# Weights' tiles at other offsets in the on-chip memory: one layer of a hybrid trunk on one core

## The chip, the cores and the metric

The kernel runs on one core of a Trainium2 chip. A core has TensorE (matrix products, results into PSUM), VectorE, ScalarE and GpSimd (elementwise work), SyncE (it issues most transfers), and SBUF, an on-chip memory of 128 partitions, in which a tile occupies the same bytes of every partition. "Offset" below is a tile's first byte in a partition, taken modulo 256. The metric is the device time of one execution in microseconds (us); the profile shows one such execution, with every instruction of every engine.

## The reference

The reference computes one layer on 1024 frames of 1024 channels, and a last RMSNorm. Cut to its large products:

```python
h = rmsnorm(x, norm_mix_g)
proj = h @ w_in                                  # 1024 -> 9248 columns
o_a = gated_delta_rule_chunked(q_a, k_a, v_a, g_a, beta_a)    # 8 heads of 128, after a short convolution
y_a = (rmsnorm(o_a, gdn_norm_g) * silu(gz)) @ w_branch_gdn
o_b = gla_chunked(q_b, k_b, v_b, log_fg)                      # 4 heads, 128 key and 256 value channels
y_b = (rmsnorm(o_b, gla_norm_g) * silu(lr)) @ w_branch_gla
x = x + (sigmoid(gate_a) * y_a + sigmoid(gate_b) * y_b) @ w_out
# cross-attention on 256 memory tokens, 4 heads of 256
x = x + (softmax(q @ k.T / 16) @ v) @ xattn_wo
x = x + square(relu(rmsnorm(x, norm_mlp_g) @ mlp_w1)) @ mlp_w2   # 4096 inner channels
return rmsnorm(x, norm_final_g)
```

All inputs and the output are float32.

## The kernel before

**Products in three steps.** Each large product is made of fp32r matmuls, a matmul form that takes float32 words. Both operands are split into a high part and a remainder, and three matmuls add up in PSUM: high x high, high x remainder, remainder x high (`mm3`, lines 493, 495 and 497). A matmul has a stationary operand of 128 x 128, loaded ahead of it by a separate weight load (PEld in the profile), and a moving operand of 512 or 256 columns that streams through. Most products go through a Strassen-Winograd scheme with seven products of half-size blocks in place of eight (`wino`, `gla_dense`).

**The weights' tiles.** A block of weights is loaded from HBM into a tile named raw. `split` (lines 531 to 534) makes its high part by a copy on ScalarE and the remainder by a subtraction on VectorE or GpSimd. The parts go into tiles of 4096 bytes a partition:

- wop, in a ring of four slots, in the pools w1 (first phases: memory keys and values, gates, GLA) and w4 (merge, output, attention, MLP);
- whi and wlo, two slots each, in the pool w2 (the delta-rule phase); wlo also in the first phase's own pool.

Four slots of a ring lie one behind the other. Every tile that is asked for under one name ("tag") takes the next slot that is free. In most products the weights are the stationary operand. In the GLA values (line 884), the folded output weights (line 711) and the scores of two of the four attention heads (line 1916) a weights' tile is the moving operand instead.

**Where tiles lie.** Pools are stacked from the left or from the right end of SBUF, and small "pad" tiles (`pad`, line 440) fill up a pool's size, so that in the built program all tiles of activations and weights of 2 KB and more have offset 0. A few others don't: gst, in which the first phase collects results for a transfer, at 96; rmb at 96; the gate weights w2g at 64; the GLA state S at 224; the identity matrix at 128.

**What sets the order.** The program is built twice. In the first pass a planner (`Plan`) takes the recorded instructions and simulates the engines with its own costs; in the second pass the order that it found is laid on each engine's queue. It takes tile sizes from `made_in` (line 449), to know which pools share memory.

Of the kernel before, what the change touches and what calls it, by code (L numbers as in the profile page):

```python
# [41 lines left out]
XO = (('K3', 'Q1', 'V0'), ('V0', 'V1', 'O2'))  # L42
LOVU = (5,)
LOV = (0, 2, 5)


def c3(t):
# [376 lines left out]
class Layer:  # L424
# [23 lines left out]

    def made_in(self, pool, shape, dt, tag, name, bufs):
        kw = {} if bufs is None else {"bufs": bufs}  # L450
        t = pool.tile(list(shape), dt, tag=tag, name=name, **kw)
        self.plan.tile(pool, tag, bufs, (t if isinstance(t, bass.AP) else t[:]).tensor.name, 4 * int(np.prod(shape[1:])))
        return t

    def psd(self):
# [1148 lines left out]

    def wino(self, bs, evicts, order=range(7), after=None, lov=LOV):

        n, ws = self.wino_w(order, lov)
        yield
        for i, p in enumerate(order):
            if i == (FW if len(ws) > 1 else 0):  # L1610
                self.fetch_w()
            for e, (w, evict) in enumerate(zip(ws, evicts)):
                x, w = bs[p], w[p]
                pt = self.psd() if (p + e) % 2 == 0 else self.pss()
                yield from self.mm3(pt, [((w[0][:, k], w[1][:, k]), (x[:, 0, k], x[:, 1, k])) for k in range(n)])
                evict(p, pt)
            if after:
                after(p)
# [360 lines left out]
    def phase_mlp(self, sp):  # L1979
# [9 lines left out]

        def up(us, order=range(7), after=None, lov=LOV):  # L1990
            puts = [self.spill(self.ad[u // 4], u % 4, nc.vector if u < 2 else None) if u < 15 else
                    lambda i, half, x: nc.sync.dma_start(self.ald[:, 2 * half + i], x) for u in us]
            return self.wino(self.mo, [self.sums(sp, relu2(put)) for put in puts],
                             order, after, lov)
# [335 lines left out]
```

## Time and profile before

| | |
|---|---|
| median of 3 runs | 2245.36 us (2243.86 to 2246.61) |
| the profiled execution | 2244.09 us |
| its span, first to last instruction | 2242.4 us |
| mean granted TensorE clock | 0.983 |
| HBM read, written | 212.35 MB, 85.75 MB |

In the profile, PE is TensorE's matmuls, PEld its weight loads, DVE VectorE, ACT ScalarE, POOL GpSimd. A group's line gives the source line, the engine, the operation, the tiles as out<-in with buffer numbers left out, and the shapes. TensorE is held by matmuls nearly throughout:

```profile
PE   7899999989899999999998999999999999999996
DVE  8835999697848858668557994558998778667756
ACT  6534554446445455355444433455675556544433
DMA  7832122122102102111167672234355445878732
```

Each digit is the busy share, in tenths, of one of 40 equal slices of the span; DMA is the mean share of the 16 DMA engines.

### The profile page before, as it was taken

To read this page: it belongs to the slowest core of one execution; us is meant where nothing else is said; L and a number is where in the kernel's file an instruction comes from. 1 tells how busy PE (TensorE), PEld (TensorE's weight loads), DVE (VectorE), ACT (ScalarE), POOL (GpSimd) and SP (SyncE) were. 2 spreads that over 40 slices of the span, in tenths; PEclk is the share of its full clock that TensorE was granted. 3 is DMA by queue.
4 is the path that set the end of the run, shared out by engine and by line. 5 is a ranking of instruction groups with operands and counts; after the bars stand their busy time and mean duration, and the time that the engine had idled before them with its cause. 6 is when DMAs were issued, how large, how long until landed. Compare 5 with 4: busy or idle time off the path is not lost.

```text
span 2242.4 us, 32240 instructions
## 1 busy us (share of the span) xinstructions
PE 2168.5 (97%) x11552; PEld 1861.4 (83%) x11552; DVE 1670.7 (75%) x2901; ACT 1106.3 (49%) x2223; POOL 369.7 (16%) x333
## 2 busy tenths in 40 slices
PE   7899999989899999999998999999999999999996
PEld 7788979878788888888886888998888888888886
DVE  8835999697848858668557994558998778667756
ACT  6534554446445455355444433455675556544433
POOL 2201112022212222121011320002331002000012
PEclk9999999999999999999999999999999999999998
DMA  7832122122102102111167672234355445878732
GB/s 257 303 132 73 58 72 72 49 74 86 62 25 93 54 29 99 38 48 67 43 215 249 213 271 90 95 132 139 125 200 167 155 155 172 275 243 283 244 122 81
DMA packets 148465, 300.23 MB, mean 134 GB/s; under 512 B 15816, under 2 KB 22344, under 8 KB 148304
## 3 DMA queue, kind: packets, MB, share of 16 engines
q1 hardware_dynamic: 141504, 289.75, 38.6%
q10 hardware_dynamic: 6800, 8.42, 1.1%
q8 instruction: 91, 1.49, 0.3%
q14 instruction: 70, 0.57, 0.1%
HBM read 212.35 MB, written 85.75 MB: 133 GB/s over the span
## 4 chain that ended last, share of the span: by engine, by line
PE 82%; DVE 10%; issue 3%; DMA 3%; ACT 2%; POOL 0%; SPq 0%; DVEq 0%; ACTq 0%; POOLq 0%
PE pd L493 19%; PE pd L495 19%; PE pd L497 19%; PE ps L495 5%; PE ps L493 5%; PE ps L497 5%; PE ps L565 2%; PE ps L1268 1%; PE ps L1259 1%; DVE Pm L1235 1%; DMA e<-obd 1%; DVE wop L534 1%; DVE pr L1233 1%; PE ps L1188 1%; PE ps L1325 1%
## 5 line engine op out<-in xcount | busy, mean ns | idle before, releaser
L533 ACT ACTIVATE wop<-raw 128x512 fp32r<-128x512 f32 (+1 forms) x444 | 297.2, 675 | 508.7 <-PE pd L497 235.9
L534 DVE TENSOR_TENSOR wop<-raw,wop 128x512 fp32r<-128x512 f32 (+1 forms) x383 | 293.6, 770 | 144.1 <-ACT wop L533 136.8
L534 POOL TENSOR_TENSOR wop<-raw,wop 128x512 fp32r<-128x512 f32 x27 | 38.8, 1438 | 389.0 <-ACT wop L533 235.5
L1129 DVE SCALAR_TENSOR_TENSOR acc<-cin,convw,acc 128x1024 f32<-128x1024 f32 x72 | 100.7, 1399 | 1.9 <-ACT acc L1127 0.7
L533 ACT ACTIVATE whi<-raw 128x512 fp32r<-128x512 f32 x86 | 52.0, 628 | 76.1 <-issue 34.8
L497 PE MATMUL pd<-t,wop 128*128 128x512 f32 x220 | 88.0, 400 | 0.0
L493 PE MATMUL pd<-t,wop 128*128 128x512 f32 x220 | 86.1, 391 | 0.8 <-ACT t L533 0.8
L495 PE MATMUL pd<-t,wop 128*128 128x512 f32 x220 | 85.9, 391 | 0.7 <-DVE t L534 0.7
L493 PE MATMUL pd<-B1a,wop 128*128 128x512 f32 (+1 forms) x220 | 82.6, 376 | 0.0
L497 PE MATMUL pd<-B1a,wop 128*128 128x512 f32 (+1 forms) x220 | 82.4, 375 | 0.0
L534 POOL TENSOR_TENSOR wlo<-raw,whi 128x512 fp32r<-128x512 f32 x29 | 45.4, 1569 | 197.7 <-ACT whi L533 143.5
L497 PE MATMUL pd<-A0a,wlo 128*128 128x512 f32 x172 | 68.8, 400 | 1.1 <-DVE wlo L534 1.1
L493 PE MATMUL pd<-A0a,whi 128*128 128x512 f32 x172 | 69.5, 404 | 0.0
L493 PE MATMUL pd<-A1b,whi 128*128 128x512 f32 x172 | 69.3, 403 | 0.0
L497 PE MATMUL pd<-A1a,wlo 128*128 128x512 f32 x172 | 68.4, 397 | 0.0
L495 PE MATMUL pd<-A1a,whi 128*128 128x512 f32 x172 | 68.3, 397 | 0.0
L497 PE MATMUL pd<-A1b,wlo 128*128 128x512 f32 x172 | 68.3, 397 | 0.0
L495 PE MATMUL pd<-A0b,whi 128*128 128x512 f32 x172 | 68.2, 396 | 0.0
L493 PE MATMUL pd<-A1a,whi 128*128 128x512 f32 x172 | 67.9, 395 | 0.0
L495 PE MATMUL pd<-A0a,whi 128*128 128x512 f32 x172 | 67.8, 394 | 0.0
L495 PE MATMUL pd<-A1b,whi 128*128 128x512 f32 x172 | 67.7, 393 | 0.0
L493 PE MATMUL pd<-A0b,whi 128*128 128x512 f32 x172 | 67.6, 393 | 0.0
(627 smaller groups left out, 7165.2 us busy)
## 6 DMA issues: line engine op xcount, KB each, us to landing
raw<-in_w_dram SPq DMA_DIRECT2D x120, 256.0 KB, 3.4
raw<-in_w_gdn_dram SPq DMA_DIRECT2D x64, 256.0 KB, 2.7
raw<-in_w_dram SPq DMA_DIRECT2D x32, 512.0 KB, 4.4
e<-ad SPq DMA_DIRECT2D x63, 256.0 KB, 4.8
ad<-q SPq DMA_DIRECT2D x45, 256.0 KB, 4.4
rawa<-ad SPq DMA_DIRECT2D x42, 256.0 KB, 4.9
A0b<-tgd SPq DMA_DIRECT2D x32, 256.0 KB, 5.8
ad<-acc SPq DMA_DIRECT2D x30, 256.0 KB, 2.4
```

What stands on the lines that cost most here:

```text
L493: nc.tensor.matmul(out, lh, rh, start=first and i == 0, stop=False)
L495: nc.tensor.matmul(out, lh, rl, start=False, stop=False)
L497: nc.tensor.matmul(out, ll, rh, start=False, stop=last and i == n - 1)
L533: nc.scalar.activation(hi, raw, AF.Copy)
L534: (lo_eng or nc.gpsimd).tensor_tensor(lo, raw, hi.bitcast(F32), SUB)
L565: self.nc.tensor.transpose(pt[:, i * P:(i + 1) * P], s, self.ident)
L1129: nc.vector.scalar_tensor_tensor(acc, cin[:, 1 + i:1 + i + T], cw[:, i:i + 1], acc, MUL, ADD)
L1188: nc.tensor.matmul(pt[:, i * P:(i + 1) * P], kc, kc, start=True, stop=True)
L1233: nc.vector.tensor_tensor(pr, X[:, c + 1:32, c:c + 1].broadcast_to([P, m, n]), Pm[:, c:c + 1, 0:n].broadcast_to([P, m, n]), MUL)
L1235: nc.vector.tensor_tensor(Pm[:, c + 1:32, 0:n], Pm[:, c + 1:32, 0:n], pr, ADD)
L1259: nc.tensor.matmul(pt[:, i * 96:(i + 1) * 96], NT[:, u + i, :], PF[:, v + i, 0:96], start=True, stop=True)
L1268: nc.tensor.matmul(pt[0:96, i * n:(i + 1) * n], PF[:, v + i, 0:96], Z, start=True, stop=True)
```

## The change

Tiles of three tags get some words more than they use: 24 (96 bytes) for wop, 16 (64 bytes) for whi and wlo. The extra words lie at a slot's end, and `made_in` returns a view of the tile without them. The planner is told the larger size.

```diff
+SHIFT = {"wop": 24, "whi": 16, "wlo": 16}
...
     def made_in(self, pool, shape, dt, tag, name, bufs):
         kw = {} if bufs is None else {"bufs": bufs}
-        t = pool.tile(list(shape), dt, tag=tag, name=name, **kw)
-        self.plan.tile(pool, tag, bufs, (t if isinstance(t, bass.AP) else t[:]).tensor.name, 4 * int(np.prod(shape[1:])))
+        n, more = int(np.prod(shape[1:])), SHIFT.get(tag, 0)
+        t = pool.tile([shape[0], n + more] if more else list(shape), dt, tag=tag, name=name, **kw)
+        self.plan.tile(pool, tag, bufs, (t if isinstance(t, bass.AP) else t[:]).tensor.name, 4 * (n + more))
+        if more and len(shape) == 3:
+            return t[:, :n].rearrange("p (a b) -> p a b", a=shape[1])
+        if more:
+            return t[:, :n].rearrange("p (a b c) -> p a b c", a=shape[1], b=shape[2])
         return t
```

The slots' distance becomes 4192 bytes for wop and 4160 for whi and wlo. In the built program the offsets are then:

| tiles | before | after |
|---|---|---|
| wop, four slots (pools w1, w4) | 0 | 64, 128, 160, 224 |
| whi, two slots (w2) | 0 | 0, 64 |
| wlo, two slots (w2) | 0 | 128, 192 |
| wlo, two slots (first phase) | 0 | 0, 64 |
| raw in w1 and w4, the input x, GLA's work tiles (ex, qk, v, sm), tiles of the first phase (acc, sq), tg of the gates' pool | 0 | 128 |
| gst, rmb | 96 | 224 |
| S, w2g | 224, 64 | 96, 192 |
| activations in A0a to B1b, t2 to t6, kv, mT, raw in w2, all tiles of the delta-rule phase of 512 bytes and more but jk | 0 | 0 |

Every engine's instructions stand in the same order as before.

## The prediction

> **What bounds the kernel now.** I read the page's busy shares first, then the chain of work that ended last.
>
> ```profile
> span 2242.4 us, 32240 instructions
> PE 2168.5 (97%) x11552; PEld 1861.4 (83%) x11552; DVE 1670.7 (75%) x2901; ACT 1106.3 (49%) x2223; POOL 369.7 (16%) x333
> PE 82%; DVE 10%; issue 3%; DMA 3%; ACT 2%; POOL 0%; SPq 0%; DVEq 0%; ACTq 0%; POOLq 0%
> ```
>
> TensorE is busy for 97% of the span and carries 82% of the chain; the transfers carry 3%. The change moves no instruction from one place to another, so the question is whether a matmul step, a split on ScalarE or VectorE, or a transfer gets longer or shorter when its operand begins at another address. Busy matmul times cannot answer that, because their ends are modelled. What can is the distance from one start to the next where nothing waits, read from the timeline of TensorE:
>
> ```profile
> 1403.16 0.39 PE L493 MATMUL pd<-B0a,wop 128*128 128x512 f32 x1
> 1403.39 0.39 PE L495 MATMUL pd<-B0b,wop 128*128 128x512 f32 x1
> 1403.61 0.39 PE L497 MATMUL pd<-B0a,wop 128*128 128x512 f32 x1
> ...
> 1405.65 0.39 PE L497 MATMUL pd<-B0a,wop 128*128 128x512 f32 x1
> 1405.88 0.39 PE L493 MATMUL pd<-B0a,wop 128*128 128x512 f32 x1
> ```
>
> The first column is the start in us. From 1403.16 to 1405.88 lie 12 steps, so a step of 512 columns is 2.72/12 = 226.7 ns. The names in front of the comma are the moving operand, the names behind it the weights. In the scores of the attention the roles turn, and a step has 256 columns:
>
> ```profile
> 1439.73 0.28 PE L495 MATMUL pd<-wop,t 128*128 128x256 f32 x1
> 1439.85 0.28 PE L497 MATMUL pd<-wop,B0a 128*128 128x256 f32 x1
> ...
> 1440.93 0.28 PE L497 MATMUL pd<-wop,B0a 128*128 128x256 f32 x1
> ```
>
> Ten steps in 1.20 us: 120 ns. So 256 more columns cost 106.7 ns (0.417 ns each), and 226.7 - 2 x 106.7 = 13.3 ns of every step do not depend on its length. In this program every operand of these matmuls begins at a multiple of 256 bytes. Counted in the built program, 7,152 steps are of the long form and 2,112 of the short one; 9,264 x 13.3 ns = 123 us of the span are this fixed part. It is the one thing in the profile that a collision between the reading of weights and the reading of the moving operand could be, and so the largest sum that the change can touch.
>
> **The change part by part.**
>
> *Order and waits.* Tile for tile, each engine issues the same instructions in the same order as before. At the head of the delta-rule phase a few small tiles now overlap the grown weights' pool of the phase before, so ScalarE and GpSimd each get one more wait ahead of an instruction, and one wait of VectorE (for two transfers) stands seven instructions earlier, ahead of the small vv at line 1174 instead of line 528.
>
> ```profile
> 529.36 0.15 DVE L1174 TENSOR_SCALAR vv<-ssk 128x8 f32<-128x8 f32 x1
> 531.88 0.17 DVE L528 TENSOR_TENSOR rs_o<-rs_y,rs_t 128x8 f32<-128x8 f32 x1
> ```
>
> What is awaited belongs to a pool that was left before this phase began, and the row of line 528 names no idle time and no releaser; I take 0. If the two transfers were late, at most the 2.5 us between these rows would be moved, with the key block of the first two heads queued behind. Bounds 0 to +2.5 us.
>
> *ScalarE and VectorE on shifted tiles.* 444 + 86 copies write hi tiles whose slots move, and in two of the three weights' pools the raw tiles that they read move to 128. Before, one tile of 2 KB, gst, begins 96 bytes past a multiple of 256; the same operation writes acc at 0:
>
> ```profile
> L533 ACT ACTIVATE wop<-raw x444: 611/632/1074, 4.0 to 2196.4; 128x512 fp32r<-128x512 f32 x131, 128x1024 fp32r<-128x1024 f32 x17
> L533 ACT ACTIVATE whi<-raw x86: 612/631/648, 493.8 to 1150.4; 128x512 fp32r<-128x512 f32 x86
> L534 DVE TENSOR_TENSOR wop<-raw,wop x383: 653/692/2315, 122.4 to 2191.7; 128x512 fp32r<-128x512 f32 x183, 128x1024 fp32r<-128x1024 f32 x9
> L715 ACT ACTIVATE gst<-pd,rs_o x16: 668/684/690, 81.5 to 131.1; 128x512 f32<-128x512 f32 x16
> L1127 ACT ACTIVATE acc<-pd,convw x48: 676/682/701, 507.4 to 1058.2; 128x512 f32<-128x512 f32 x48
> L701 DVE TENSOR_TENSOR gst<-pd,rmb x32: 406/410/426, 47.3 to 79.5; 128x256 f32<-128x256 f32 x32
> L686 DVE TENSOR_TENSOR kv<-pd,kv x16: 402/417/425, 17.4 to 122.1; 128x256 fp32r<-128x256 f32 x16
> ```
>
> Medians of 684 against 682 ns on ScalarE, and 410 against 417 on VectorE, where rmb is read and gst written off the grid and kv on it. The price is 0 to +2 ns a split; 530 x 2 ns = 1 us of engines that are 49% and 75% busy, and the copies of a unit are made while TensorE is on the one before. I take 0.
>
> *The moving operand off the grid.* The words ahead of the change say that the moving operands stay at 0. That holds for the long steps with activations as moving operand, but not everywhere: in the GLA values, the folded output weights and the scores of two heads the weights' tiles are themselves the moving operand; by the built program 1,136 steps stream from a shifted slot. One plain-fp32 matmul of before streams from an address 224 bytes past the grid (S in the GLA scan, line 1007), beside others that stream v from 0 with the same weights' shape:
>
> ```profile
> 486.30 0.59 PE L1005 MATMUL ps<-v,ex 128*128 128x256 f32 x2
> 486.73 0.59 PE L1007 MATMUL ps<-S,qk 128*128 128x256 f32 x2
> 487.16 0.59 PE L1003 MATMUL ps<-v,ex 128*128 128x256 f32 x2
> 487.59 0.59 PE L1005 MATMUL ps<-v,ex 128*128 128x256 f32 x2
> ```
>
> Each pair of records takes 0.43 us, whichever address it streams from. Bounds: 0 by this row, and one more fixed part (13.3 ns x 1,136 = 15 us) if the doubled rate of the fp32r stream has no slack left. I take 0.
>
> *The weights off the grid.* This is the main term. 6,352 long steps and 576 short ones load their weights from a slot that isn't at 0. The nearest row is again plain fp32: w2g, a stationary tile 64 bytes past the grid.
>
> ```profile
> 209.83 1.88 PE L931 MATMUL ps<-sm,w2g 96*128 96x512 f32 x4
> L931 PE MATMUL ps<-sm,w2g x16: 590/592/594, 209.8 to 435.2; 96*128 96x512 f32 x16
> ```
>
> Four records last 1.88 us from the first start to the last end, and one lasts 0.592, so three steps take 1.29 us: 0.43 us a step of 512 columns. The rows at 486 us give 0.43/2 = 0.215 us for 256 columns with weights at 0. Twice 0.215 is 0.43: within the 10 ns of these columns, shifted weights add nothing. The same rows speak against a gain: 256 columns at twice 0.417 ns are 213 ns, so with both operands at 0 plain fp32 pays only about 2 ns of fixed part a step. Equal residues alone therefore don't make the 13.3 ns; the fp32r form does.
>
> Bounds for a shifted step, then: -13.3 ns (the whole fixed part is a collision and goes) to +13.3 ns (the load takes twice its fixed part); 6,928 x 13.3 = 92 us either way. I take 0, by the nearest row.
>
> [...]
>
> *Transfers.* The raw tiles of two pools, x and the GLA work tiles now begin 128 past the grid. [...] From the chain's row alone: 3% of 2242 us are 67 us, and raw tiles are a part of it; I bound this at 0 to +4 us, one sixteenth, and take 0, because the weights are fetched several units ahead.
>
> **Sum.** 0 for each part. The profiled execution took 2244.1 us (span 2242.4 and 1.7 around it); the median of the runs is 2245.4, with 2.7 us between lowest and highest. I predict 2245 us.
>
> **Rivals.**
>
> *Slower: a load from an odd multiple of 32 bytes costs more.* Two of the four wop slots lie at 160 and 224. If such a load touches a row of the memory more than an aligned one, its fixed part grows; for half as much again, 6.7 ns, 2,464 long and 240 short steps give 18 us: 2263; for twice, 36 us: 2281. It decides from about 2 ns a load on, because these steps follow each other without a gap. With every shifted slot dear it is 92 us: 2337. [...] Against it: the w2g row, though at 64, never at an odd 32.
>
> *Slower by little: transfers, or the 1,136 streamed steps.* 4 to 15 us: 2249 to 2260.
>
> *Faster: the fixed part is a collision.* For it: it is constant, in both forms, and every operand sits at the same residue. If it goes on all 6,928 steps, 92 us x 82% of the chain = 76 us: 2169; if only where the residues differ enough, a part of that. Against it: the plain-fp32 rows, and that the step stays at 226.7 wherever in its tile the weights begin.
>
> *The change doesn't do what it says* (the slots stay where they were) I can exclude by the built program's addresses.
>
> **How the numbers follow.** No change 42% (2241 to 2249 its own range). Slower 40%: 32% by the loads, 8% by the small terms; it is given much weight because the only rows for a shifted operand are of another number form. Faster 18%. A difference below 0.2%, 4.5 us, can't be told from no change here. The range reaches up to a load twice as dear plus some of the small terms, 2290, and down to a fifth of the collision, 2228; I leave out about 8% above and 10% below.
>
> **What would show it.** Right: the step of long runs stays at 226.7 ns in all slots, and 120 ns in the scores. The slower rival: steps of two sizes that follow the slots in turn, the longer in the slots at 160 and 224. The faster one: steps below 226, down to 213. Transfers: a longer time to landing of raw and a larger share of DMA in the chain. A change of ScalarE's 632 ns or VectorE's 692 ns for a split would prove the second part wrong.

## The result and the profile after

The kernel with the shifted tiles takes 2275.88 us (median of 4 runs, 2271.52 to 2276.36) against 2245.57 us of the kernel before (4 runs, 2243.86 to 2246.61). The ratio is 1.0131, 95% interval 1.0114 to 1.0149: slower by 30 us. The likeliest case of the prediction, no change, did not come; the measured time lies in its range, near the rival of a dearer weight load.

The page of the changed kernel, its span, busy times and the chain's shares by engine:

```profile
span 2273.8 us, 32242 instructions
PE 2199.6 (97%) x11552; PEld 1856.5 (82%) x11552; DVE 1674.4 (74%) x2901; ACT 1106.3 (49%) x2223; POOL 373.7 (16%) x333
PE 87%; DVE 7%; issue 3%; ACT 2%; DMA 1%; POOL 1%; DVEq 0%; SPq 0%; ACTq 0%; POOLq 0%
```

The span grew by 31.4 us, TensorE's busy time by 31.1 us with the same 11,552 matmuls; ScalarE's didn't move and VectorE's grew by 3.7 us. TensorE's share of the chain went from 82 to 87%, that of VectorE and the transfers fell. The mean granted clock is 0.986, before 0.983, so the throttle isn't the cause. From `made_in` on, line numbers stand six higher: lines 493, 495 and 497 are now 499, 501 and 503, and the copies of `split` are lines 539 and 540.

The timeline of TensorE shows it directly. This is a run of long steps whose weights lie in the wop slot at 160 (columns as in the prediction: start, duration, engine, line, moving operand, weights):

```profile
1630.20 0.39 PE L499 MATMUL pd<-A1b,wop 128*128 128x512 f32 x1
1630.42 0.40 PE L501 MATMUL pd<-A1b,wop 128*128 128x512 f32 x1
1630.66 0.39 PE L503 MATMUL pd<-A1b,wop 128*128 128x512 f32 x1
1630.89 0.39 PE L499 MATMUL pd<-A1b,wop 128*128 128x512 f32 x1
...
1632.76 0.39 PE L503 MATMUL pd<-A1b,wop 128*128 128x512 f32 x1
1632.99 0.39 PE L499 MATMUL ps<-B1b,wop 128*128 128x512 f32 x1
```

Twelve steps from 1630.20 to 1632.99 take 2.79 us, 232.5 ns each; the steps of the kernel before took 226.7. Nothing waits between them.

To see which steps grew, each matmul record of the trace was set beside the instruction of the built program, which knows the addresses. The next table counts long steps between steps of their own kind, at full clock, by the start of the weights loaded during the step less the start of the operand that streams, modulo 256 (27 steps at 32 are not in it):

| weights less moving operand | steps | mean ns, changed kernel |
|---|---|---|
| 0 | 581 | 231.1 (most common values 234 and 227) |
| 64 | 1,731 | 233.0 |
| 128 | 1,517 | 232.0 |
| 160 | 1,193 | 233.7 |
| 192 | 301 | 229.9 |
| 224 | 1,204 | 233.3 |
| kernel before: 0 throughout | 6,558 | 227.0 |

A row at 0 also holds steps right behind a tile at another offset, hence its two values. So no slot off 0 is spared, and 64 is as dear as 160. That 256 is the period, the kernel before shows: taken modulo 4096, its differences lie at all sixteen multiples of 256, and the mean step at each is 226.8 to 227.3 ns. Matched step for step with the kernel before, the time between two long steps grew by 37.5 us in all, 5.6 ns for each of 6,733. The other side of the account: steps of 256 columns lost 3.2 us (before 119.9 ns each, now 117.9 to 119.3 on average where the offsets differ), the distances in which a long step follows a wait gained 1.4 us, and all other distances and waits of TensorE lost 5.3. That sums to 30.4 of the span's 31.4 us; the last 1 us lies ahead of the first matmul.

The growth sits where the long steps are. From 1472 us to the end (attention's output and the MLP) 2,968 of them gave 18.3 us, 6.2 ns each; in the delta-rule phase, 497 to 1170 us, 1,762 gave 7.2 us, 4.1 ns each.

### The profile page after: what moved, and what is told of

It reads as the page before. It is cut to its first block, busy times and chain, and to the rows that moved or that the text cites. A ratio compares the mean times of both kernels' runs of the same rounds, so it can differ in the third digit from the quotient of the medians.

```text
span 2273.8 us, 32242 instructions
## 1 busy us (share of the span) xinstructions
PE 2199.6 (97%) x11552; PEld 1856.5 (82%) x11552; DVE 1674.4 (74%) x2901; ACT 1106.3 (49%) x2223; POOL 373.7 (16%) x333
## 4 chain that ended last, share of the span: by engine, by line
PE 87%; DVE 7%; issue 3%; ACT 2%; DMA 1%; POOL 1%; DVEq 0%; SPq 0%; ACTq 0%; POOLq 0%
PE pd L501 20%; PE pd L503 20%; PE pd L499 20%; PE ps L501 5%; PE ps L499 5%; PE ps L503 5%; PE ps L571 2%; PE ps L1274 1%; PE ps L1265 1%; DVE Pm L1241 1%; PE ps L1194 1%; PE ps L1331 1%; PE ps L1208 1%; PE ps L1314 1%; DVE pr L1239 1%
## 5 line engine op out<-in xcount | busy, mean ns | idle before, releaser
L501 PE MATMUL pd<-B0b,wop 128*128 128x512 f32 x172 | 68.1, 396 | 1.4 <-DVE B0b L540 1.4
L499 PE MATMUL pd<-A1b,whi 128*128 128x512 f32 x172 | 69.4, 403 | 0.0
L501 PE MATMUL pd<-A1a,whi 128*128 128x512 f32 x172 | 69.0, 401 | 0.0
L503 PE MATMUL pd<-A0b,wlo 128*128 128x512 f32 x172 | 68.8, 400 | 0.0
```

Source lines behind the costliest of these rows:

```text
L499: nc.tensor.matmul(out, lh, rh, start=first and i == 0, stop=False)
L501: nc.tensor.matmul(out, lh, rl, start=False, stop=False)
L503: nc.tensor.matmul(out, ll, rh, start=False, stop=last and i == n - 1)
```

## The experiments

All kernels of this section are the kernel before with other places for some tiles. Each chosen tag gets 64 words more, and a view of it begins `k` words (4k bytes) into the slot; slots then lie a multiple of 256 bytes apart, so that all slots of a tag have one offset. Each engine keeps its order of instructions. A ratio is that to the kernel before, run beside it, with its 95% interval in brackets. The theories that they tell apart:

- A: what counts is where the weights begin relative to the operand that streams while they are loaded, modulo 256. Equal is cheap.
- B: what counts is the absolute offset of an operand; 0 is cheap, whatever the other one does.
- C: the distance of the slots (4192, 4160 bytes) or the larger pools are to blame.
- D: a ring whose slots have different offsets, the change from one to the next, is to blame.
- E: the tiles that moved along (raw, x, the GLA tiles) are to blame, through transfers or copies.

**The larger slots alone.**

```diff
+OFF = {"wop": 0, "whi": 0, "wlo": 0}
...
     def made_in(self, pool, shape, dt, tag, name, bufs):
+        n = int(np.prod(shape[1:]))
+        k = OFF.get(tag)
+        room = 0 if k is None else 64
+        t = pool.tile([shape[0], n + room] if room else list(shape), dt, tag=tag, name=name, **kw)
...
+        t = t[:, k:k + n]
```

> The slots of wop, whi and wlo grow by 256 bytes and every tile keeps offset 0. Theory A (what counts is where the weights begin relative to the moving operand, modulo 256) and theory B (a load of weights from anywhere but a multiple of 256 is dearer) both expect the long step at 226.7 ns and 2245 us. Rival C (the slots' other distance, no longer a multiple of 4096, is what costs) expects about 2275 us.

Measured: 2245.66 us (10 runs, 2244.26 to 2249.27), ratio 1.0004 [0.9994, 1.0014]. The long step is 227.0 ns. The slots now lie 4352 bytes apart, and neither that nor the room costs anything; C falls.

**All weights' tiles at 128, nothing else.**

```diff
-OFF = {"wop": 0, "whi": 0, "wlo": 0}
+OFF = {"wop": 32, "whi": 32, "wlo": 32}
```

> Slots as in the run before, but every weights' tile begins 128 bytes into its slot; all else stays at 0. Theories A and B expect long steps of about 232 ns, as the changed kernel shows at 128, and 2270 to 2278 us. Rival D (it is the mixture of offsets, one slot after another, that costs) expects 226.7 ns and 2245 us.

Measured: 2273.72 us (4 runs, 2272.71 to 2275.24), ratio 1.0129 [1.0114, 1.0144]. One offset for all slots, an even multiple of 64, and the whole loss is there. That takes D away, and also the prediction's rival, which asked for odd multiples of 32. From the timeline of TensorE in this kernel, where lines 504, 506 and 508 are the three matmuls of `mm3`:

```profile
1636.15 0.40 PE L508 MATMUL pd<-B1b,wop 128*128 128x512 f32 x1
1636.38 0.40 PE L504 MATMUL pd<-B1b,wop 128*128 128x512 f32 x1
...
1639.17 0.39 PE L504 MATMUL pd<-t,wop 128*128 128x512 f32 x1
1639.40 0.40 PE L506 MATMUL pd<-t,wop 128*128 128x512 f32 x1
```

From 1636.15 to 1639.40 are 14 steps: 232.1 ns. Over all 6,555 such steps the mean is 232.4.

**Weights and activations at 128 together.** This is the run that decides between A and B: both operands of the large products are as far off 0 as the weights of the last one, and equal to each other.

```diff
-OFF = {"wop": 0, "whi": 0, "wlo": 0}
+OFF = {"wop": 32, "whi": 32, "wlo": 32, "A0a": 32, "A0b": 32, "A1a": 32, "A1b": 32, "B0a": 32, "B0b": 32, "B1a": 32, "B1b": 32, "t2": 32, "t4": 32, "t6": 32, "mT": 32, "kv": 32}
```

> The weights' tiles and the activations that meet them in fp32r matmuls all begin at offset 128. Theory A expects 226.7 ns again and 2245 us, since both are shifted alike. Theory B expects 232 ns and about 2275 us.

Measured: 2242.09 us (10 runs, 2240.78 to 2247.10), ratio 0.9990 [0.9981, 1.0000]. The loss is gone. On TensorE's timeline:

```profile
1639.79 0.39 PE L508 MATMUL ps<-B1b,wop 128*128 128x512 f32 x1
1640.02 0.39 PE L504 MATMUL ps<-B1b,wop 128*128 128x512 f32 x1
...
1642.74 0.39 PE L504 MATMUL pd<-A1a,wop 128*128 128x512 f32 x1
1642.96 0.39 PE L506 MATMUL pd<-A1a,wop 128*128 128x512 f32 x1
```

From 1639.79 to 1642.96 are 14 steps: 226.4 ns; the mean over 6,563 is 227.1. B falls: 128 is as good as 0 when both operands have it.

**The moving operands alone at 128.** The weights stay at 0, as far from the moving operand as above, from the other side.

```diff
-OFF = {"wop": 0, "whi": 0, "wlo": 0}
+OFF = {"A0a": 32, "A0b": 32, "A1a": 32, "A1b": 32, "B0a": 32, "B0b": 32, "B1a": 32, "B1b": 32, "t2": 32, "t4": 32, "t6": 32, "mT": 32, "kv": 32}
```

> The mirror image of the run with the weights at 128: the activations begin at 128, all weights' tiles at 0. Theory A expects the long step at about 232 ns and 2270 to 2278 us, as there. Theory B expects 226.7 ns where the weights are the stationary operand, and 2245 us within 3 us.

Measured: 2277.35 us (4 runs, 2276.53 to 2279.53), ratio 1.0136 [1.0117, 1.0156]. On TensorE's timeline:

```profile
1640.22 0.40 PE L504 MATMUL pd<-B1b,wop 128*128 128x512 f32 x1
1640.46 0.40 PE L506 MATMUL pd<-B1b,wop 128*128 128x512 f32 x1
...
1643.01 0.39 PE L504 MATMUL pd<-t,wop 128*128 128x512 f32 x1
1643.24 0.40 PE L506 MATMUL pd<-t,wop 128*128 128x512 f32 x1
```

13 steps from 1640.22 to 1643.24, 232.3 ns each; the mean over 6,552 is 232.4, as with the weights shifted. The weights were not touched here, so it is no property of the load by itself. A stands.

**The tiles beside them, alone.** raw, the input x and GLA's work tiles ex, qk and sm begin at 128, weights and activations at 0.

```diff
-OFF = {"wop": 0, "whi": 0, "wlo": 0}
+OFF = {"raw": 32, "x": 32, "ex": 32, "qk": 32, "sm": 32}
```

> Only the tiles that the change moved by the way go to 128: raw, x and GLA's ex, qk and sm; weights and activations stay at 0. Theories A and B expect 226.7 ns and 2245 us. Rival E (loads and copies of those tiles get dearer) expects a part of the 30 us: 2250 us or more.

Measured: 2246.01 us (10 runs, 2243.89 to 2249.89), ratio 1.0001 [0.9992, 1.0011]. E falls for these tiles. The others that moved along in the change (v, the first phase's tiles, tg, gst, rmb, S, w2g) keep their places here; but in the run with the weights at 128 all of them lay as in the kernel before, and the whole loss was there.

**A map over all offsets.** The weights' tiles take the offsets 0, 16, 32 and so on to 240 in turn, four tiles of a tag each; the activations stay at 0.

```diff
+SEEN = {}
...
         k = OFF.get(tag)
+        if k is not None:
+            i = SEEN[id(self), tag] = SEEN.get((id(self), tag), -1) + 1
+            k = 4 * (i // 4 % 16)
```

> Each fourth weights' tile in turn begins 16 bytes further in its slot: 0, 16, 32 and so on to 240, all else at 0. It measures the step at 16 offsets in one run. Theory A expects a curve with its one low point at 0 (226.7 ns) among the long steps. A rule by 32 or 64 bytes (a load off such a boundary is dearer) expects equal steps at all multiples of 64 and longer ones between. The change itself showed 232 to 234 ns at 64, 128, 160 and 224.

Measured, one execution: 2270.76 us. Means of the long steps, from 317 to 524 of them for each offset, by weights less moving operand:

| offset | 0 | 16 | 32 | 48 | 64 | 80 | 96 | 112 |
|---|---|---|---|---|---|---|---|---|
| ns | 228.4 | 229.5 | 233.0 | 232.3 | 233.1 | 231.8 | 234.1 | 233.1 |

| offset | 128 | 144 | 160 | 176 | 192 | 208 | 224 | 240 |
|---|---|---|---|---|---|---|---|---|
| ns | 233.2 | 233.3 | 233.2 | 230.2 | 229.2 | 233.2 | 232.9 | 227.7 |

At 0, 16 and 240 the most common step is 227 ns; their means are raised by steps that follow another tile. 176 and 192 lie between. Everything else costs 5 to 7 ns, with no period of 64 or 32. Near-equal starts are cheap, all others but 176 and 192 are about alike.

A speaks of the weights that are loaded during the step; the map doesn't single them out. A step that streams at an equal start takes 226.9 ns when the weights loaded during it have an equal start too (385 steps). When those lie elsewhere it takes 233.1 (125 steps). But when the step's own weights lie elsewhere and those loaded during it are equal, it takes 233.0 as well (130 steps). So a pair of operands is shown to count, and not which of the two loads makes the step longer.

**The same map for the products of 256 columns alone**, to see whether the short steps gain what the changed kernel's trace seemed to show.

```diff
-OFF = {"wop": 0, "whi": 0, "wlo": 0}
+OFF = {"wop": 0, "wlo": 0}
+SEEN = {}
...
+        if k is not None and shape[-1] == 256:
+            i = SEEN[id(self), tag, len(shape)] = SEEN.get((id(self), tag, len(shape)), -1) + 1
+            k = 4 * (i // 2 % 16)
```

> Only the weights' tiles of the products with steps of 256 columns are shifted, each pair by 16 bytes more; the long steps keep offset 0 on both sides. Theory A expects 226.7 ns for every long step, and for the short ones a curve of its own over the offset, at most places 1 to 3 ns under the 120 ns of offset 0, as the changed kernel shows (118 ns), 5 ns under it at the best. The time: 2240 to 2246 us. Theory B expects short steps of 120 ns and more.

Measured, one execution: 2247.43 us, with the kernel before at 2243.90 beside it. Short steps at equal offsets are 119.6 ns, at each other offset from 117.2 to 119.1: 0.5 to 2.4 ns shorter, but one execution can't show so little in the whole. The next kernel is the one that was timed for it.

**Short steps 64 apart, timed.** The tiles of the 256-column products (1,696 steps) move by 64 bytes, so that they differ from their partners; all long steps stay equal.

```diff
-OFF = {"wop": 0, "whi": 0, "wlo": 0}
+OFF = {"wop": 0, "B0b": 0}
...
+        if k is not None and shape[-1] == 256:
+            k = 16
```

> A trial for a version faster than both: only the weights' tiles of steps with 256 columns begin at 64 (as moving operand in the GLA values and the scores, as weights in the memory projections), all else at 0. Theory A expects 226.7 ns for the long steps and 118 ns in place of 120 for about 1,700 short ones, so 3 us less if nothing else takes them: 2242 us. That the short steps are covered by other waits would give 2245 us.

Measured: 2243.42 us (12 runs, 2236.02 to 2246.24), ratio 0.9988 [0.9980, 0.9996]. The moved steps are 117.3 to 118.1 ns; 1,696 times 2 ns is 3.4 us, and the median is 2.8 us below that of the kernel before. Small, but the interval is clear of 1.

**The delta-rule phase alone at 128**, to see whether its waits hide a part of the loss (a sixth theory, F).

```diff
-OFF = {"wop": 0, "whi": 0, "wlo": 0}
+OFF = {"whi": 0, "wlo": 0}
...
+        if k is not None and tuple(shape) == (P, NB, P):
+            k = 32
```

> Only the weights of the delta-rule phase (whi, wlo) go to 128, 2,064 long steps. Theory A by the step alone, 5.7 ns each as with all weights at 128, expects 12 us more: 2257 us. Rival F (this phase has gaps in which TensorE waits for VectorE's substitution, and long steps there were already irregular before) expects less than half of it: 2247 to 2251 us.

Measured: 2252.03 us (11 runs, 2248.01 to 2255.45), ratio 1.0025 [1.0016, 1.0034], 5.8 us more. That is just under half of A's 12, as F expected, though the time lies 1 us above F's. In its profile the distances between two long steps of the phase grew by 8.3 us (1,763 of 4.7 ns, not 2,064 of 5.7), those behind a wait by 1.5, and other steps and waits there gave 3.6 back. So a part of the 12 was over-counted and a part was absorbed.

**Both gains in one kernel.** Weights and activations at 128 as above, and the tiles of the 256-column products at 192.

```diff
-OFF = {"wop": 0, "whi": 0, "wlo": 0}
+OFF = {"wop": 32, "whi": 32, "wlo": 32, "A0a": 32, "A0b": 32, "A1a": 32, "A1b": 32, "B0a": 32, "B0b": 32, "B1a": 32, "B1b": 32, "t2": 32, "t4": 32, "t6": 32, "mT": 32, "kv": 32}
...
+        if tag in ("wop", "B0b") and shape[-1] == 256:
+            k = 48
```

> The kernel of e3_both_128 with the tiles of the 256-column products (wop, and B0b where it has 256 columns) another 64 bytes further, at 192, so that 1,696 short steps have weights 64 away from their moving operand as in e8_short_64, and all long steps have equal offsets. Theory A with the short steps' gain as e8 showed it: long step 227, the shifted short steps 1 to 2 ns shorter than 120, and the time 2 to 3 us below that of e3: 2238 to 2242, ratio to the kernel before about 0.998. Rival: the 0.1% of e3 and that of e8 are chance or don't add: 2242 to 2246, ratio 0.999 or above.

Measured: 2239.37 us (8 runs, 2235.70 to 2241.78), ratio 0.9974 [0.9963, 0.9984]. This beats the kernel before by 0.26%, the best of all kernels here. In the scores of two heads, on TensorE's timeline (lines 506, 508 and 510 are now `mm3`):

```profile
1436.63 0.28 PE L506 MATMUL pd<-wop,t 128*128 128x256 f32 x1
1436.75 0.28 PE L508 MATMUL pd<-wop,t 128*128 128x256 f32 x1
...
1438.87 0.28 PE L508 MATMUL pd<-wop,t 128*128 128x256 f32 x1
1438.99 0.28 PE L510 MATMUL pd<-wop,B0a 128*128 128x256 f32 x1
```

20 steps from 1436.63 to 1438.99: 118.0 ns, where the prediction's rows of the same product gave 120. The long steps stay at 227.1 on average. Matched with the kernel before, the 256-column steps lost 5.0 us (2.1 from 175 to 497 us), the plain-fp32 steps of the delta-rule phase about 3.

## Why the prediction was wrong

**The weights off the grid** is the step that failed: "I take 0, by the nearest row". The rows were plain fp32, w2g at 64 and the S product, and the prediction carried them over to fp32r. They were read rightly. But in the change both operands of each row moved by 128, so that their difference stayed: w2g lies 64 past sm before and after, and qk lies 32 past S modulo 256. The S product of the kernel before, and then both groups in the changed kernel:

```profile
L1007 PE MATMUL ps<-S,qk x56: 379/379/483, 268.2 to 490.4; 128*128 128x256 f32 x56
L937 PE MATMUL ps<-sm,w2g x16: 590/592/595, 209.8 to 435.9; 96*128 96x512 f32 x16
L1013 PE MATMUL ps<-S,qk x56: 378/379/483, 267.9 to 491.8; 128*128 128x256 f32 x56
```

Medians of 592 and 379 ns are those of before. What they show is only that plain fp32 doesn't care where such a pair lies as a whole. For its difference there is one comparison: 256 columns take 215.7 ns at equal starts (215.6 in the changed kernel) and 215.9 at a difference of 32 (in both kernels). What failed is the inference. The prediction itself had noted that such a step has next to no fixed part ("the fp32r form does"), so it could not bear witness on what happens to that part. In fp32r the long step grew from 226.7 to 232.4 ns with the weights at 128. In the changed kernel the 6,733 distances between long steps grew by 5.6 ns on average, which made 37.5 us of the bound of 92.

**"It is the one thing in the profile that a collision ... could be"**, the fixed part of 13.3 ns, is not borne out either. In the kernel with the weights at 128 the short steps whose starts are 128 apart take 118.8 ns on average. Worked out in the prediction's way, 232.4 - 118.8 is 113.6 ns for 256 columns (0.444 ns each, before 0.417) and leaves a fixed part of 5 ns in place of 13.3. Two lengths can't say how a step is made up, but that its fixed part grew isn't shown, nor that the 13.3 ns are a weight load.

**The bounds and the rivals.** The bound held, and the size of the rival "half as much again" was right for a step: 6.7 ns against the measured 5 to 7. Its place was wrong. It was to strike only 160 and 224; 64 and 128 cost the same, and with the weights left at 0 and the activations moved (2277.35 us) the loss is there too. So it is neither an odd 32 nor the load, but the pair. That the measured 2276 us lie between this rival's 2263 and 2281, and in the range, is luck: it made 2,704 steps longer, and 6,733 distances grew. The rival "faster", a collision between two operands at equal residues, had the right idea, that it is a matter between the two operands, with the wrong sign for long steps: the equal residue is the good case. For the short steps its sign was right, at 2 ns instead of 13.3.

**"Equal residues alone therefore don't make the 13.3 ns"** stands for its plain-fp32 rows, with about 2 ns of fixed part by its estimate, but the prediction drew from it that residues don't matter.

**The moving operand off the grid** was taken as 0 with a bound of +15 us. The short steps among the 1,136 got shorter by 1 to 2 ns. That is a gain, and the bounds had left gains out without a reason; TensorE's steps of 256 columns lost 3.2 us in the changed kernel.

**ScalarE and VectorE on shifted tiles: 0**, right. Copies and subtractions of the changed kernel:

```profile
L539 ACT ACTIVATE wop<-raw x444: 612/632/1070, 4.0 to 2227.6; 128x512 fp32r<-128x512 f32 x131, 128x1024 fp32r<-128x1024 f32 x17
L539 ACT ACTIVATE whi<-raw x86: 612/630/647, 495.2 to 1157.6; 128x512 fp32r<-128x512 f32 x86
L540 DVE TENSOR_TENSOR wop<-raw,wop x383: 654/692/2321, 120.1 to 2222.7; 128x512 fp32r<-128x512 f32 x183, 128x1024 fp32r<-128x1024 f32 x9
```

Medians of 632, 630 and 692 ns against 632, 631 and 692.

**Transfers: 0**, right. In the changed kernel the time to landing is

```profile
raw<-in_w_dram SPq DMA_DIRECT2D x120, 256.0 KB, 3.6
```

against 3.4 before, but the kernel with the weights at 128, whose raw stays at 0, shows the same 3.6. The bound of 4 us, which is also the low end of the rival "slower by little", takes one sixteenth of the chain's 67 us; no run shows that share. What the runs show in its place: with raw, x and GLA's tiles moved alone the kernel took 2246.01 us, and the ratio of 1.0001 [0.9992, 1.0011] leaves at most 2.5 us for it.

**Order and waits: 0**, right: none of the waits of TensorE, the engine that sets the end, grew by more than 1.2 us, and all its waits of this view together are 64.5 us before and 64.7 after. The longest, of the changed kernel's waits (line waiting, line waited for, us in total, times, longest), is

```profile
PE ps L1265 <- ACT PF L1251: 17.1, 4, 7.1
```

and it was 18.6 us before.

**The two operands together.** The four kernels with weights, activations, both or neither at 128 measured 2273.72, 2277.35, 2242.09 and 2245.66 us, their long steps 232.4, 232.4, 227.1 and 227.0 ns: the time of an fp32r step depends on the starts of both operands together.

**Still open.** What in the memory the two reads share, or whether it is the memory at all, no run shows; only the dependence on the two starts is shown. Nor do the runs tell why the short step gains where the long one loses, or why 176 and 192 are about half as dear. The kernel with weights and activations at 128 is 3 us faster than the one before, and plain-fp32 steps of its delta-rule phase took about 2.4 us less; but its interval touches 1, and the cause wasn't isolated.

## What to carry to other kernels

Give the stationary and the moving operand of long fp32r matmuls starts that are equal modulo 256 bytes, at 0 or, as measured here too, at 128 (227.0 and 227.1 ns a step); in this kernel, where TensorE sets the end, most other differences cost 5 to 7 ns in 227 for each 512-column step, 1.3% of the time. Before a row is used as witness for an operation, see that it is of the same form and that the change in question happens in it: plain fp32 had next to no fixed part (an estimated 2 ns, from rows of 215 ns), and the two operands of its rows moved together. A cost or gain of a pair of operands is found by moving each alone and both together, three runs that here settled what no single shift could.

## What the runs showed of the hardware that was not expected

- An fp32r step of 512 columns depends on the two operands' starts relative to each other: 227 ns where they are equal modulo 256, 232.4 at a difference of 128, 227.7 to 234.1 over the fifteen other differences of the map. The steps are then uneven, single ones from 226 to 241 ns in repeating patterns.
- Steps of 256 columns react the other way: 119.9 ns at equal starts, 117.2 to 119.1 at others (one product with 45 steps in the map of all tiles came to 113.7). Setting them apart gave 0.1% (0.9988 [0.9980, 0.9996]). With all long steps' operands at 128 as well it was 0.26%; the short steps lost 5.0 us in that profile.
- Steps of plain fp32 with 256 columns took 215.7 ns at equal starts and 215.9 at a difference of 32; larger differences were not tried at that length.
